# SWA's division and turning rearranged around two transposes for the last 64 keys, with narrower roots in the last norm

## The chip, the cores and the metric

The kernel runs on one core of a Trainium2 chip. The metric is the device time of one execution in microseconds. The engines are PE (TensorE, matrix products and transposes), DVE (VectorE), ACT (ScalarE), POOL (GpSimd) and SP (SyncE, which here only starts DMAs).

## The reference, cut to what matters

One step of a one-layer encoder over 1024 prompt tokens and 64 sample tokens, width 1024, in float32. The layer adds three things to the input: a mix of retention (four heads) and sliding-window attention (SWA), cross-attention to 256 memory tokens, and a SwiGLU block. A last RMS norm follows. The parts that the change touches:

```python
def swa_attend(q, k, v, bias, sinks, valid):
    s = jnp.einsum('bnqhgd,bnkhd->bnhgqk', q, k) * (SWA_HD ** -0.5) + bias
    s = jnp.where(valid, s, NEG_INF)
    m = jnp.maximum(jnp.max(s, axis=-1, keepdims=True), sink)
    e = jnp.exp(s - m)
    p = e / (jnp.sum(e, axis=-1, keepdims=True) + jnp.exp(sink - m))
    return jnp.einsum('bnhgqk,bnkhd->bnqhgd', p, v)
...
y_prompt, y_sample = rms_norm(hp, g_final), rms_norm(hs, g_final)
```

SWA has 16 query heads and 2 kv heads of 64 columns each. A chunk is 64 tokens, and its queries see 192 keys: their own chunk and the two before. Each row of exps is divided by its sum, and the weighted values follow.

## The kernel before, in words

Tokens lie along the free dimension (1088 columns), features along the 128 partitions. A product of full precision is made of three passes over high and low halves of the numbers (L156, L157, L158). The phases run one after the other: the projections and retention (to 811 us), SWA with the output projection of retention in its gaps (811 to 1007), the merge of the two branches (to 1110), cross-attention (to 1400), SwiGLU and the last norm (to 2209). A scheduler orders the instructions of each engine at build time. The code steers it with `issue_after` (this instruction stands behind that one), `in_order` (behind the last product) and, in the last norm, `queued` (DVE's instructions stand in the order of the code).

**SWA** (`swa`, L924 on). 17 chunks of 64 queries; the last is the sample's. A chunk is worked in two halves, so there are 34. The tile `t` of a half has 128 rows of queries and four blocks: two kv heads `v` by two groups of query heads `i`. From the third chunk on a block has 192 keys. A half passes through three steps.

- `scores`: products into two PSUM banks `pss` (L969). DVE adds the bias (L979, L982 in the first two chunks), takes the maximum (L984), turns it into the negative one `nm` (L985) and into the sinks' exponent `es` (L988). ACT takes four exps with their sums `den` (L990) and the sinks' (L992). DVE adds these (L993) and takes the reciprocal (L994). One POOL instruction divides all four blocks, 768 elements a partition (L996).
- `turn`: PE turns the first 128 keys of the four blocks into one bank (L1008), and ACT copies it to `pT` (L1012). PE then turns the last 64 keys in four transposes (L1018). Two of them take 64 columns, and two take 128 columns, the keys 64 to 191, to land on the upper partitions. DVE copies the result (L1020).
- `weigh`, once per chunk: four products of 512 columns (L1031), two for the first 128 keys with 128 rows by 64 columns of the array, two for the last 64 keys with 64 by 64. They add up in one bank `pout`. DVE copies it to `osb` (L1035), and SP stores that.

The order of the code is: `weigh` of the half before, `scores` of two halves ahead, `turn` of this half, and then pieces of the filler. The filler (`filler`, L1146) projects retention's output by `w_ret_out` in half pieces of 12 products. DVE multiplies a finished piece by the gate (L1187). PSUM has eight banks. The pool `pd` of the filler, which also takes the values' transposes (L946, copied by ACT at L948), has three; `pss` has two, and the two turned tiles and `pout` have one each. Weights come in by DMA as `raw` and are split into high and low by ACT (L123) and DVE (L124).

**The last norm** (`finish`, L1620). The last 16 products make the columns 0 and 1, each 272 tokens, of eight row blocks; columns 2 (544 tokens) are complete before. Per product DVE adds it to `y` (L1639), ACT squares that (L1643), and DVE gathers the squares (L1648). For the columns 2 and 0 the sums over the features come from tiny products with tokens on the partitions (`sums`, L1656), so that the roots (`steps`, L1721 to L1726) work on 5 or 3 elements a partition. PE spreads the factors over the partitions again (`spread`, L1682), and ACT copies them (L1685). For the columns 1 `wide_roots` makes the sums on all partitions at once (L1670, L1671), and the same steps work on 272 elements. Each scaling (L1689) is one DVE instruction, followed by a store from SP (L120).

## Time and profile before

| What | Value |
|---|---|
| Median of three runs | 2211.39 us (2210.66 to 2214.1) |
| The profiled execution | 2210.58 us |
| Its span | 2208.8 us |
| Mean granted clock of PE | 0.992 |
| PE busy in SWA (811 to 1007) | 186.9 of 196 us |
| DVE busy there | 143.0 us |
| POOL busy there | 53.7 us |
| PE busy from 2176 to 2208 | 16.5 of 32 us |

The profiled execution's own time is 1.8 us more than its span, the stretch from the first to the last recorded instruction. A line of the timeline has the start in us, the duration in us, the engine, the source line, the operation, the tiles written and read, the shapes and the count of the instructions drawn together. Brackets hold the idle time of the engine ahead of it and what ended that. A line of a group has the count, busy time in us and mean duration in ns.

### The profile page before, as it was taken

To read this page: it belongs to the slowest core of one execution; us is meant where nothing else is said; L and a number is where in the kernel's file an instruction comes from. 1 tells how busy PE (TensorE), PEld (TensorE's weight loads), DVE (VectorE), ACT (ScalarE), POOL (GpSimd) and SP (SyncE) were. 2 spreads that over 40 slices of the span, in tenths; PEclk is the share of its full clock that TensorE was granted. 3 is DMA by queue.
4 is the path that set the end of the run, shared out by engine and by line. 5 is a ranking of instruction groups with operands and counts; after the bars stand their busy time and mean duration, and the time that the engine had idled before them with its cause. 6 is when DMAs were issued, how large, how long until landed. Compare 5 with 4: busy or idle time off the path is not lost.

```text
span 2208.8 us, 41446 instructions
## 1 busy us (share of the span) xinstructions
PE 2155.7 (98%) x16307; PEld 2089.8 (95%) x16307; DVE 1577.8 (71%) x2654; ACT 875.8 (40%) x1894; POOL 653.2 (30%) x442
## 2 busy tenths in 40 slices
PE   8999999999999998999999999999999999999996
PEld 8999999999999996779999999999999999999996
DVE  7996958776677668775455555768777776778498
ACT  7344424344344346553133333333322222344243
POOL 1322333332343122230000000014555555544440
PEclk9999999999999999999999999999999999999998
DMA  5534253445245476327443111422333332385233
GB/s 197 167 127 137 90 149 122 131 127 156 96 153 172 165 220 213 112 64 224 124 153 107 57 49 58 144 86 90 124 133 101 104 118 95 124 297 167 91 114 110
DMA packets 181444, 290.83 MB, mean 132 GB/s; under 512 B 40290, under 2 KB 109314, under 8 KB 181250
## 3 DMA queue, kind: packets, MB, share of 16 engines
q1 hardware_dynamic: 176706, 278.74, 39.5%
q10 hardware_dynamic: 4032, 7.80, 0.9%
q8 instruction: 129, 2.11, 0.4%
q0 software_dynamic: 512, 1.64, 0.2%
q14 instruction: 65, 0.53, 0.1%
HBM read 196.95 MB, written 91.16 MB: 130 GB/s over the span
## 4 chain that ended last, share of the span: by engine, by line
PE 80%; DVE 11%; DMA 4%; ACT 2%; issue 2%; POOL 1%; SPq 0%; DVEq 0%; ACTq 0%; POOLq 0%
PE pq L215 15%; PE pq L212 15%; PE pq L213 15%; PE pd L156 8%; PE pd L158 8%; PE pd L157 8%; DVE wq L124 1%; PE pout L1031 1%; PE pss L969 1%; DMA hl<-d_op 1%; DVE T L124 1%; DVE B L124 1%; PE pp L1008 1%; DMA qs<-d_qkv 1%; DVE stage L596 1%
## 5 line engine op out<-in xcount | busy, mean ns | idle before, releaser
L124 DVE TENSOR_TENSOR wq<-raw,wq 128x512 fp32r<-128x512 f32 (+1 forms) x499 | 441.2, 888 | 137.1 <-ACT wq L123 135.5
L123 ACT CAST wq<-raw 128x512 fp32r<-128x512 f32 (+1 forms) x499 | 303.6, 614 | 586.0 <-PE pq L215 244.8
L212 PE MATMUL pq<-T,wq 128*128 128x272 f32 x1832 | 490.8, 288 | 3.6 <-ACT wq L123 2.1
L213 PE MATMUL pq<-T,wq 128*128 128x272 f32 x1832 | 491.5, 288 | 0.0
L213 PE MATMUL pq<-B,wq 128*128 128x272 f32 x1592 | 429.6, 290 | 6.7 <-DVE B L124 6.7
L212 PE MATMUL pq<-B,wq 128*128 128x272 f32 x1592 | 427.4, 289 | 1.3 <-DVE stage L596 1.1
L215 PE MATMUL pq<-T,wq 128*128 128x272 f32 x1832 | 382.0, 289 | 0.9 <-DVE wq L124 0.9
L190 POOL TENSOR_TENSOR raw<-raw 128x512 f32<-128x512 f32 (+1 forms) x59 | 90.2, 1529 | 967.1 <-DVE rs_r L301 480.4
L212 PEld LDWEIGHTS pq<-T,wq 128*128 128x128 f32 x1832 | 344.1, 188 | 5.6 <-ACT wq L123 1.9
L213 PEld LDWEIGHTS pq<-T,wq 128*128 128x128 f32 x1832 | 344.1, 188 | 0.8 <-issue 0.7
L215 PE MATMUL pq<-B,wq 128*128 128x272 f32 x1592 | 332.8, 289 | 0.0
L213 PEld LDWEIGHTS pq<-B,wq 128*128 128x128 f32 x1592 | 300.7, 189 | 9.2 <-DVE B L124 8.3
L212 PEld LDWEIGHTS pq<-B,wq 128*128 128x128 f32 x1592 | 300.5, 189 | 1.8 <-ACT wq L123 1.3
L215 PEld LDWEIGHTS pq<-T,wq 128*128 128x128 f32 x1832 | 289.6, 189 | 1.6 <-DVE wq L124 1.1
L215 PEld LDWEIGHTS pq<-B,wq 128*128 128x128 f32 x1592 | 252.8, 190 | 0.8 <-issue 0.8
L259 DVE TENSOR_TENSOR u<-pq,u 128x544 f32<-128x544 f32 x177 | 127.5, 720 | 101.3 <-PE pq L215 100.4
L193 POOL TENSOR_TENSOR raw<-raw 128x512 f32<-128x512 f32 (+1 forms) x59 | 82.8, 1403 | 110.4 <-DVE wq L124 105.3
L596 DVE TENSOR_TENSOR stage<-pq,u 128x544 f32<-128x544 f32 x112 | 80.4, 718 | 34.6 <-PE pq L215 31.2
L191 POOL TENSOR_TENSOR raw<-raw 128x512 f32<-128x512 f32 (+1 forms) x59 | 90.4, 1533 | 3.5
L996 POOL TENSOR_TENSOR t<-t,den 128x768 f32<-128x768 f32 (+2 forms) x34 | 49.9, 1468 | 127.0 <-DVE den L994 51.9
L196 POOL TENSOR_TENSOR raw<-raw 128x512 f32<-128x512 f32 (+1 forms) x59 | 82.4, 1397 | 4.4
L990 ACT ACTIVATE t<-t,nm 128x192 f32<-128x192 f32 (+2 forms) x136 | 58.9, 434 | 45.5 <-DVE nm L985 45.5
(388 smaller groups left out, 4600.4 us busy)
## 6 DMA issues: line engine op xcount, KB each, us to landing
hl<-d_op SPq DMA_DIRECT2D x85, 272.0 KB, 4.7
d_qkv<-stage SPq DMA_DIRECT2D x44, 272.0 KB, 2.2
d_op<-stage SPq DMA_DIRECT2D x44, 272.0 KB, 2.1
d_op<-ht SPq DMA_DIRECT2D x44, 272.0 KB, 3.3
raw<-w_gate SPq DMA_DIRECT2D x22, 512.0 KB, 3.5
raw<-w_up SPq DMA_DIRECT2D x22, 512.0 KB, 3.7
raw<-w_down SPq DMA_DIRECT2D x16, 512.0 KB, 4.1
d_gate<-stage ACTq DMA_DIRECT2D x28, 272.0 KB, 2.9
```

The lines of the kernel that those rows point to most:

```text
L123: self.last_cast = self.nc.scalar.copy(hi, src).ins
L124: return self.nc.vector.tensor_tensor(out=lo, in0=src, in1=hi.bitcast(F32), op=ALU.subtract).ins
L156: mm(ps, wh, xh, start=start, stop=False)
L157: mm(ps, wh, xl, start=False, stop=False)
L158: self.last_mm = mm(ps, wl, xh, start=False, stop=stop).ins
L190: tt(out=a11, in0=a11, in1=a21, op=sub)
L191: tt(out=a21, in0=a21, in1=a22, op=add)
L212: mm(ps[:, c, :HC], w[:, 0, ks], x[:, 0, cs], start=start, stop=False)
L213: mm(ps[:, c, :HC], w[:, 0, ks], x[:, 1, cs], start=False, stop=False)
L215: self.last_mm = mm(ps[:, c, :HC], w[:, 1, ks], x[:, 0, c * HC:(c + 1) * HC], start=False, stop=stop).ins
L259: add = lambda out, a, b: nc.vector.tensor_tensor(out=out, in0=a, in1=b, op=ALU.add)
L596: nc.vector.tensor_tensor(out=o, in0=ps, in1=sb, op=ALU.add)
```

## The change

**SWA.** The dense pool `pd` has two banks during SWA and three again from the merge on; `pout` has two. The division becomes three POOL instructions in a half of full width. The first takes the first 128 keys of all four blocks in place. The other two, one per kv head, take the last 64 keys and write them to a new tile `e`, in which the two kv heads lie side by side (in the second half of a chunk the other way round). Two transposes of 128 by 128 turn `e` where four turned the last 64 keys. `weigh` has four products of 256 columns for each of its two parts, and each half `h` of the columns has a bank of its own. The second part uses the four 64-by-64 quadrants of the array. In the filler, the load and the split of the third unit of `w_ret_out` stand behind the gating of the first piece.

**The last norm.** `wide_roots` goes. The sums of the columns 1 come from tiny products, and the last product's squares are added by a second product instead of a gather. The steps then work on three elements a partition, with one scaling of the columns 0 between them. The factors of the columns 0 and 1 are read where PE spread them, in PSUM. One row block of the columns 2 and three of the columns 1 get their gain from ACT and their factor from POOL (`gain`, `aside`). The last eight stores alternate between SP's and ACT's queue.

```diff
                 self.project_phase()
+                with self.plain_psum(2, side="right"):
+                    self.swa_phase()
                 with self.plain_psum(side="right"):
-                    self.mix_phase()
+                    self.merge_swa()
                     self.mem.close()
...
     @contextmanager
-    def plain_psum(self, **where):
+    def plain_psum(self, bufs=3, **where):
         with ExitStack() as ctx:
-            pd = ctx.enter_context(self.tc.tile_pool(name="pd", bufs=3, reuse_waits="tile", space=PSUM, **where))
+            pd = ctx.enter_context(self.tc.tile_pool(name="pd", bufs=bufs, reuse_waits="tile", space=PSUM, **where))
             self.dense_psum = lambda: pd.tile([P, 512], F32, tag="d", name="pd")
...
 
-    def mix_phase(self):
+    def swa_phase(self):
         with ExitStack() as ctx:
...
             self.swa(ctx, fill())
-        self.merge_swa()
 
...
                 nc.vector.reciprocal(den, den)
-                p = lambda x: x.rearrange("p v i n -> p (v i) n")
-                nc.gpsimd.tensor_tensor(out=p(t)[:, :, :nk], in0=p(t)[:, :, :nk], op=ALU.mult,
-                                        in1=den.rearrange("p v i -> p (v i)").unsqueeze(2).broadcast_to([P, 4, nk]))
-                live[c, hf] = t
+                p, n, e = t.rearrange("p v i n -> p (v i) n")[:, :, :min(nk, P)], min(nk, P), None
+                nc.gpsimd.tensor_tensor(out=p, in0=p, op=ALU.mult,
+                                        in1=den.rearrange("p v i -> p (v i)").unsqueeze(2).broadcast_to([P, 4, n]))
+                if nk == NKEY:
+                    e = sw.tile([P, 2, 2, 64], F32, tag="e", bufs=4, name="e")
+                    for v in range(2):
+                        nc.gpsimd.tensor_tensor(out=e[:, :, v ^ hf, :], in0=t[:, v, :, P:], op=ALU.mult,
+                                                in1=den[:, v, :].unsqueeze(2).broadcast_to([P, 2, 64]))
+                live[c, hf] = t, e
 
...
                     live[c] = [values(ks + k0) for k0 in ((0, 64, P) if nk == NKEY else (0,))]
-                t, vt = live.pop((c, hf)), live[c]
+                (t, e), vt = live.pop((c, hf)), live[c]
                 n = min(P, nk)
...
                 nc.scalar.copy(pT[:, :, hf * 256:(hf + 1) * 256], pp[:n, :].rearrange("p (v i) -> p v i", v=2))
-                parts = [[(vt[0][:n], pT[:, v, :]) for v in range(2)]]
+                cs = [slice(h * 256, (h + 1) * 256) for h in range(2)]
+                parts = [[(h, v, vt[0][:n], pT[:, v, cs[h]]) for h in range(2) for v in range(2)]]
                 if nk == NKEY:
                     pp = pw.tile([P, 512], F32, tag="pt1", name="pp")
-                    for v, i in reversed(units):
-                        k0, n = (64, P) if v else (P, 64)
-                        self.last_mm = nc.tensor.transpose(pp[:n, i * P:(i + 1) * P], t[:, v, i, k0:k0 + n], self.ident).ins
+                    for i in range(2):
+                        x = e[:, i].rearrange("p r k -> p (r k)")
+                        self.last_mm = nc.tensor.transpose(pp[:, i * P:(i + 1) * P], x, self.ident).ins
                     pT = live[c, "T"][1]
                     nc.vector.tensor_copy(pT[:, hf * 256:(hf + 1) * 256], pp[:, :256])
-                    parts.append([(vt[2 - v][rows[v]], pT[rows[v]]) for v in range(2)])
+                    parts.append([(h, r ^ h, vt[2 - r][rows[r]], pT[rows[r], cs[h]]) for h in range(2) for r in (h, 1 - h)])
                 live[c, "parts"] = parts
...
                 parts = live.pop((c, "parts"))
-                po = pw.tile([P, 512], F32, tag="out", name="pout")
+                po = pw.tile([P, 2, 512], F32, tag="out", name="pout")
                 for j, part in enumerate(parts):
-                    for v, (val, pT) in enumerate(part):
-                        self.last_mm = mm(po[rows[v], :], val[:, rows[v]], pT, start=j == 0, stop=j == len(parts) - 1).ins
+                    for h, v, val, pT in part:
+                        self.last_mm = mm(po[rows[v], h, :256], val[:, rows[v]], pT, start=j == 0, stop=j == len(parts) - 1).ins
                 if c % 2 == 0:
...
                 osb = outs["osb"]
-                nc.vector.tensor_copy(osb[:, :, c % 2, :], po.rearrange("p (m q) -> p m q", q=64))
+                nc.vector.tensor_copy(osb[:, :, c % 2, :].rearrange("p (h m) q -> p h m q", h=2),
+                                      po[:, :, :256].rearrange("p h (m q) -> p h m q", q=64))
                 if c % 2 == 1 or c == 16:
...
                 if m not in units:
-                    units[m] = self.unit(io["w_ret_out"][m], KT)
+                    if m == 2:
+                        with tc.issue_after(first):
+                            units[m] = self.unit(io["w_ret_out"][m], KT)
+                    else:
+                        units[m] = self.unit(io["w_ret_out"][m], KT)
                 u, g = units[m], ld()
...
                         yield
-                nc.vector.tensor_tensor(out=g[:, :n], in0=ps, in1=g[:, :n], op=ALU.mult)
+                ins = nc.vector.tensor_tensor(out=g[:, :n], in0=ps, in1=g[:, :n], op=ALU.mult).ins
+                if step == 2:
+                    first = ins
                 self.store(self.d_mix[m, :, c0:c0 + n], g[:, :n])
...
 
-        def sums(c):
+        def sums(c, *more):
 
...
             ps = bank()[:, :2 * len(spans)].rearrange("p (t two) -> p t two", two=2)
+            parts = [self.rstd[:, cols[c]], *more]
             for i, (a, w) in enumerate(spans):
-                a += cols[c].start
-                self.last_mm = nc.tensor.matmul(ps[:, i, :], self.rstd[:, a:a + w], self.ones[:, :2], start=True, stop=True).ins
+                for j, x in enumerate(parts):
+                    self.last_mm = nc.tensor.matmul(ps[:, i, :], x[:, a:a + w], self.ones[:, :2], start=j == 0,
+                                                    stop=j == len(parts) - 1).ins
             r = self.np.tile([P, 5], F32, tag="rf", bufs=2, name="rs_f")[:, :len(spans)]
...
 
-        def roots(c):
+        def roots(c, between=None):
             r, spans, ps = factors[c]
...
             t = self.np.tile([P, 5], F32, tag="tf", bufs=2, name="rf_t")[:, :len(spans)]
-            self.steps(r, v, t, ps)
-
-        def wide_roots(c, m):
+            self.steps(r, v, t, ps, between)
 
-            ps = bank()[:, :HC]
-            mm = nc.tensor.matmul
-            mm(ps, self.ones, self.rstd[:, cols[c]], start=True, stop=False)
-            self.last_mm = mm(ps, self.ones, squares[c, m], start=False, stop=True).ins
-            v, t = (self.hl.tile([P, HALF], F32, tag="hl", name="wide")[:, :HC] for _ in range(2))
-            self.steps(self.rstd[:, cols[c]], v, t, ps)
-
-        def spread(c):
+        def spread(c, copied=True):
             r, spans, _ = factors[c]
...
                 c0 = cols[c].start
-                nc.scalar.copy(self.rstd[:, c0 + a0:c0 + a1], pb[:, :a1 - a0])
+                if copied:
+                    nc.scalar.copy(self.rstd[:, c0 + a0:c0 + a1], pb[:, :a1 - a0])
+            return pb
+
+        def scale(c, k, by=None, queue=nc.sync):
+            o = y[k][:, cols[c]]
+            by = self.rstd[:, cols[c]] if by is None else by
+            self.queued(lambda: stt(o, o, self.gains[:, 3, k:k + 1], by, ALU.mult, ALU.mult))
+            queue.dma_start(self.io["o_y"][k, :, cols[c]], o)
 
-        def scale(c, k):
+        def gain(c, k):
             o = y[k][:, cols[c]]
-            self.queued(lambda: stt(o, o, self.gains[:, 3, k:k + 1], self.rstd[:, cols[c]], ALU.mult, ALU.mult))
-            self.store(self.io["o_y"][k, :, cols[c]], o)
+            nc.scalar.mul(o, o, self.gains[:, 3, k:k + 1])
+
+        def aside(c, k, queue=nc.sync):
+            o = y[k][:, cols[c]]
+            nc.gpsimd.tensor_tensor(out=o, in0=o, in1=self.rstd[:, cols[c]], op=ALU.mult)
+            queue.dma_start(self.io["o_y"][k, :, cols[c]], o)
 
...
             if j == KT + 6:
-                self.in_order(lambda: spread(0))
-            if j >= KT:
-                scale(2, j - KT)
-        for k in range(3):
-            scale(0, k)
-        self.in_order(lambda: wide_roots(1, rest[-1][0]))
+                pb0 = self.in_order(lambda: spread(0, False))[:, :HC]
+            if c and m < KT - 1:
+                scale(2, m)
+            if c and KT - 5 < m < KT - 1:
+                gain(1, rest[m][0])
+            if j == 2 * KT - 2:
+                gain(2, KT - 1)
+                aside(2, KT - 1)
+        m = rest[-1][0]
+        spare = [rest[i][0] for i in range(KT - 4, KT - 1)]
+        scale(0, 0, pb0)
+        scale(0, 1, pb0)
+        self.in_order(lambda: sums(1, squares[1, m]))
+        roots(1, lambda: scale(0, 2, pb0))
         for k in range(3, KT):
-            scale(0, k)
-        for k in range(KT):
-            scale(1, k)
+            scale(0, k, pb0)
+        pb = self.in_order(lambda: spread(1))[:, :HC]
+        queues = [nc.sync, nc.scalar]
+        rows = [k for k in range(KT) if k not in spare]
+        for i, k in zip((2, 4, 7), spare):
+            rows.insert(i, k)
+        for i, k in enumerate(rows):
+            if k in spare:
+                aside(1, k, queues[i % 2])
+            else:
+                scale(1, k, pb, queues[i % 2])
 
-    def steps(self, out, v, t, ps):
+    def steps(self, out, v, t, ps, between=None):
         nc = self.nc
...
         nc.scalar.activation(out, v, AF.Sqrt)
+        if between is not None:
+            between()
         q(lambda: nc.vector.reciprocal(out, out))
```

In the built order of the instructions, POOL has three instructions per half of full width instead of one, PE two transposes instead of four and eight products per `weigh` instead of four. L1187 of the first piece stands ahead of the two splits of the third unit on DVE, and the transposes of the last values (L946) stand behind the last `turn`. In the merge, the first products that read the seventh operand stand six products earlier on PE. DVE's order within a chunk is as it was.

## The prediction

> **What bounds the kernel now.** The page comes first, for the bound of the whole.
>
> ```profile
> span 2208.8 us, 41446 instructions
> ## 1 busy us (share of the span) xinstructions
> PE 2155.7 (98%) x16307; PEld 2089.8 (95%) x16307; DVE 1577.8 (71%) x2654; ACT 875.8 (40%) x1894; POOL 653.2 (30%) x442
> ```
>
> PE is busy for 98% of the span. A change pays only if it takes PE time away, or time in which PE has nothing to do. Two stages matter, so the busy times by stretch come next: the steady part of the sliding-window attention (SWA), and the tail behind the last product.
>
> ```profile
> 880.00:1000.00 120.00, 120.00 (x788) 90.67 (x787) 86.48 (x194) 65.92 (x253) 34.83 (x23) 1.00 0.30 92
> 2193.00:2208.00 15.00, 1.18 (x4) 0.68 (x4) 11.32 (x24) 0.86 (x2) 0.00 (x0) 0.59 0.54 186
> ```
>
> The columns are the stretch, its length, then PE, PEld, DVE, ACT and POOL busy, the granted clock and the DMA share. From 880 to 1000 PE never stops, while DVE works 86.5 of 120 us and POOL 34.8. From 2193 on PE does 1.18 us in 15 and DVE sets the time. The copy of the weighted values, once per chunk, gives the period of the loop:
>
> ```profile
> L1035 DVE COPY osb<-pout x12: 680/692/693, 881.5 to 993.7; 128x512 f32<-128x512 f32 x12
> ```
>
> Twelve copies, 112.2 us from first to last: 10.2 us per chunk of two halves, bound by PE.
>
> **SWA, what PE saves.** The timeline of PE at one turn:
>
> ```profile
> 908.90 2.09 PE L1031 MATMUL pout<-pT,swin 128*64 128x512 f32 x8
> 910.92 0.92 PE L969 MATMUL pss<-swin,swin 64*128 64x192 f32 x8
> 911.77 0.33 PE L946 MATMUL pd<-ident,swin 128*128 128x128 f32 x1
> 911.94 0.60 PE L1008 MATMUL pp<-ident,t 128*128 128x128 f32 x4
> 912.37 0.60 PE L1018 MATMUL pp<-ident,t 128*128 128x128 f32 x4
> 912.73 0.42 PE L156 MATMUL pd<-ret,wq 128*128 128x384 f32 x1
> ```
>
> Four transposes of L1008 take 0.43 us from start to start (911.94 to 912.37), so one is 0.11, and two fewer in L1018 save 0.22 per half, 0.44 per chunk. The weighing takes 2.02 us (908.90 to 910.92) in two parts of 1.01, each two tiles side by side. The second part becomes four products of 256 columns on the four 64x64 quadrants. If they run two by two, they cost what they cost now, or up to 0.2 more if each start costs as between these rows; if all four run at once the part falls by 0.43. PE alone would so allow 10.2 − 0.44 = 9.76 us per chunk, or 9.33.
>
> At this place a rule of the Trainium skill speaks against the sum (TensorEngine Tiling (Array Packing), Restrictions and Gotchas): different row tiles may not use one PSUM bank at the same time. The two tiles of the second part before are of different row halves, write one bank, and yet took 1.01 us for two passes of 512 columns each, as the first part did; the trace doesn't show the rule for different partitions of a bank. After, each half of the columns has a bank of its own. By the rule the second part would run two by two; without it, all four.
>
> **SWA, what the loop allows.** The last-64-key transposes now wait for the third of three POOL operations. Prices of the division:
>
> ```profile
> L996 POOL TENSOR_TENSOR t<-t,den 128x768 f32<-128x768 f32 x30 | 45.6, 1521 | 106.8 <-DVE den L994 34.3 <-DVE nm L985 30.1 <-PE pss L969 17.9
> L996 POOL TENSOR_TENSOR t<-t,den 128x512 f32<-128x512 f32 x2 | 2.4, 1192 | 15.0 <-DVE den L994 15.0
> L996 POOL TENSOR_TENSOR t<-t,den 128x256 f32<-128x256 f32 x2 | 1.9, 947 | 5.2 <-DVE den L994 2.7 <-DVE es L988 2.6
> ```
>
> 256 elements cost 0.95, 512 cost 1.19, 768 cost 1.47 undisturbed: about 1.08 ns an element on 0.64 us. An operation of 128 elements isn't in the trace; between nothing less than the 0.64 and the 0.95 of 256, I take 0.77, on the line. The three are then 1.19 + 2 × 0.77 = 2.73 us, with gaps some 2.84, against 1.47: 1.4 later than now.
>
> ```profile
> 904.84 0.45 ACT L990 ACTIVATE t<-t,nm 128x192 f32<-128x192 f32 x1 [1.37 <-DVE nm L985]
> ...
> 908.44 1.73 POOL L996 TENSOR_TENSOR t<-t,den 128x768 f32<-128x768 f32 x1 [4.54 <-DVE den L994]
> ...
> 908.76 1.43 DVE L985 SCALAR_TENSOR_TENSOR nm<-nm,minus 128x4 f32<-128x4 f32 x1
> ...
> 914.99 0.46 ACT L990 ACTIVATE t<-t,nm 128x192 f32<-128x192 f32 x1 [1.77 <-DVE nm L985]
> ```
>
> The loop of one half: exps (904.84) to the division (908.44) are 3.60; the three operations 2.84; then the second transposes, the copy L1020, and behind it on DVE L984, L985 and the exps of the half two later, 2.62 us (912.37 to 914.99). Sum 9.06 us, below the 9.76 of PE, without one thing: L985, with two inputs in SBUF, took 1.43 us instead of about 0.16 (914.73, in the rows after these, started 0.26 ahead of its exps) and ended at 910.19, just when POOL did (908.44 + 1.73 = 910.17). So a DVE operation of two SBUF inputs waits for a POOL operation that is running. Does it wait for all three? Here is a waiting one with a second POOL operation queued:
>
> ```profile
> 325.25 1.30 POOL L191 TENSOR_TENSOR raw<-raw 128x512 f32<-128x512 f32 x1
> ...
> 325.86 1.24 DVE L124 TENSOR_TENSOR wq<-raw,wq 128x512 fp32r<-128x512 f32 x1 [0.58 <-ACT wq L123]
> ...
> 326.51 1.81 POOL L602 TENSOR_TENSOR stage<-stage,rstd 128x544 f32<-128x544 f32 x1
> ```
>
> L191 ends at 326.55, L124 at 327.10 and L602 at 328.32: DVE got in between, and POOL waited. So L985 waits at most for the one that runs, 0 to 1.19; with hits in about a third of the chunks' time I add 0.4: loop 9.5, still below 9.76. The Trainium skill says the same of the lock (SBUF — State Buffer, Who interferes with whom): it is held for one instruction, and the other blocks. I take PE as the bound with a small part of the quadrants' overlap: 0.5 us per chunk (between −0.2 and 0.87), **12 chunks, −6.0**. The first chunks are bound by other things and get nothing.
>
> **SWA, the edges.** At halves 4 and 33 nothing lies between the division and the turn:
>
> ```profile
> 848.63 1.47 POOL L996 TENSOR_TENSOR t<-t,den 128x768 f32<-128x768 f32 x1 [4.11 <-DVE den L994]
> ...
> 850.15 0.66 PE L1008 MATMUL pp<-ident,t 128*128 128x128 f32 x4
> ...
> 995.48 1.47 POOL L996 TENSOR_TENSOR t<-t,den 128x768 f32<-128x768 f32 x1 [2.65 <-DVE den L994]
> ...
> 997.00 0.66 PE L1008 MATMUL pp<-ident,t 128*128 128x128 f32 x4
> ```
>
> The second transposes come 0.43 behind L1008, at 850.59 and 997.44; after, they could start at 848.63 + 2.84 + 0.05 = 851.52 and 998.37. **+0.9 each, +1.9.** Behind them in PE's queue stands the filler, which waits with them.
>
> The dense pool has two tiles instead of three, so a piece waits for the copy of the piece before the last. Once per some pieces that is late:
>
> ```profile
> 914.89 0.34 PE L156 MATMUL pd<-ret,wq 128*128 128x384 f32 x1
> ...
> 915.09 0.56 DVE L1187 TENSOR_TENSOR swin<-pd,swin 128x384 f32<-128x384 f32 x1
> ```
>
> This piece starts 0.8 before the other has been read (915.65). Four tiles of 38 are late in this way, by 0.3 to 0.8: **+1.5** (0.5 to 3).
>
> At the start PE stands 4.0 us, because DVE's queue waits for weights:
>
> ```profile
> PE pss L969 <- DVE t L982: 4.0, 1, 4.0
> ```
> ```profile
> 829.71 1.14 ACT L123 CAST wq<-raw 128x512 fp32r<-128x512 f32 x2 [7.25 <-DMA raw<-w_ret_out]
> ...
> 831.57 0.55 DVE L1187 TENSOR_TENSOR swin<-pd,swin 128x384 f32<-128x384 f32 x1
> ```
>
> L1187 of the first piece moves ahead of the splits that wait for that cast, so L982 behind it comes 0.55 earlier: **−0.5**. The casts on ACT stay where they are, so the wait itself remains.
>
> In the merge the scheduler puts the products with the seventh SWA operand 6 matmuls earlier. Its cast comes just in time now:
>
> ```profile
> 1027.58 1.86 ACT L123 CAST swa<-ld 128x320 fp32r<-128x320 f32 x4 [2.41 <-DMA ld<-d_swa]
> ...
> 1028.92 0.69 PE L156 MATMUL pd<-swa,wq 128*128 128x384 f32 x3
> ```
>
> Six matmuls are 1.0 us at 0.17 each: **+0.8** (0 to 1.5). SWA in sum: −6.0 + 1.9 + 1.5 − 0.5 + 0.8 = **−2.3**.
>
> **The finish.** Narrow factors as the trace shows them for columns 0, then the wide ones and the scales:
>
> ```profile
> 2185.33 0.73 PE L1656 MATMUL pq<-ones,rstd 128*128 128x2 f32 x6
> ...
> 2186.71 0.16 DVE L1721 TENSOR_SCALAR rf_v<-pq 128x3 f32<-128x3 f32 x1
> ...
> 2187.75 0.16 DVE L1726 SCALAR_TENSOR_TENSOR rs_f<-rf_t,rs_f 128x3 f32<-128x3 f32 x1
> ```
> ```profile
> 2193.55 0.73 PE L1670 MATMUL pq<-rstd,ones 128*128 128x272 f32 x2 [2.18 <-DVE rstd L1648]
> ...
> 2195.34 0.44 DVE L1721 TENSOR_SCALAR wide<-pq 128x272 f32<-128x272 f32 x1
> ...
> 2199.12 0.44 DVE L1726 SCALAR_TENSOR_TENSOR rstd<-wide,rstd 128x272 f32<-128x272 f32 x1
> 2199.48 2.15 DVE L1689 SCALAR_TENSOR_TENSOR y<-y,gains,rstd 128x272 f32<-128x272 f32 x5
> ...
> 2202.88 3.38 SPq L120 DMA_DIRECT2D o_y<-y  x7
> ```
>
> Before: sums from 2193.55, roots 2195.34 to 2199.56, then 13 scales at 0.41 (five in 2.15 less the last's overlap), the last store issued by 2206, the end 2.9 later. After: the sums start by 2193.8 (POOL's `aside` of (2,7) holds one L1648 by the lock, 0.3 to 0.5), twelve tiny products cost 2 × 0.73, so the roots start at 2195.4; the narrow steps take 1.2 (2186.71 to 2187.91), with one scale between them 1.7 to 1.9: 2197.3. The spread is 3 tiny products and the wait, 0.9: 2198.2. Beside it DVE does the other five scales of columns 0, 2197.3 to 2199.35. Left are five scales with the factor in PSUM, 2.1 us, to 2201.5; three rows go to POOL at some 0.93 each (272 elements on the line above) from 2198.8, when ACT's copy is there, to 2201.7. Two queues issue the stores, 0.48 each (3.38 for 7), so the last goes at 2201.8 and the end comes 2.9 later at 2204.7 instead of 2208.8: **−4.1** (−2.5 to −5.0). That a DVE scale with its factor in PSUM costs no more than one in SBUF isn't shown; L1639, which reads PSUM, takes the same 0.44 for 272 elements. The lower end is for POOL being held by DVE.
>
> **Sum.** −2.3 − 4.1 = −6.4 on the profiled execution's 2210.6 gives 2204.2. That execution lay 0.8 below the median of 2211.4, so **2205**.
>
> **Rivals.** (a) All four quadrants run at once and the second transposes are never late: 0.87 per chunk, −10.4 for SWA's loop; with the rest unchanged −10.8, 2200.6, and 2196 if the first chunks gain too. For it: two column tiles and two row tiles each do run side by side in the rows above. Against it: the loop of 9.5 would then be longer than PE's 9.33. (b) The new weighing costs its starts (0.2 per chunk) or the loop eats the saving, and the two-buffer and merge terms are at their upper ends: −3 + 1.9 + 3 − 0.5 + 1.5 − 4.1 = about −1, and with a finish of −2.5 about 0: 2208 to 2212. In this case the change does what it says, and the saved transposes don't arrive on the path. (c) Slower: the lock. If L985 waits for all of the POOL operations behind each other, not for one, each loop gets 1.27 more, and L993, of two SBUF inputs too, 0.77: 9.06 + 2.04 = 11.1, which is 0.9 above today's 10.2. Then the loop's term is +10.8 instead of −6.0: 2222. It decides from a loop of 10.6 on (12 × 0.4 = 4.8, which with +3.7 of edges and −4.1 of the finish is 4.4). Against it stand the rows at 325 us.
>
> **Chances.** Forecast (2201.5 to 2207) 0.52, (a) 0.20, (b) 0.17, (c) 0.11. The range 2197 to 2213 leaves out (c) and the far end of (a). A measurement of this kernel can tell about 0.2%, 4.4 us, from no change: faster means below 2207.0, slower above 2215.8. Faster holds (a) and nearly all of the forecast, 0.68; same 0.21; slower 0.11.
>
> **What the profile after would show.** The two L1018 transposes at 0.11 each and a period of L1035 near 9.7; L985 at 0.16 or up to 1.2, never 2; the sum of the three divisions near 2.8; no PE wait on POOL's `e` but at two halves; PE's waits for L1187 or L948 summing to about 1.5; the second part of the weighing at 1.0 (two by two) or 0.55 (four). In the finish, the narrow L1721 near 2195.4, the last DVE scale near 2201.5, the end 4 us earlier. The forecast falls if PE waits for POOL or L1020 in every chunk, or if the tail's last store goes out later than 2203.

## The result, and the profile after

The changed kernel takes 2199.95 us (median of four runs, 2197.7 to 2201.3) against 2212.1 us for the kernel before, whose four runs lie between 2210.66 and 2214.1. The ratio is 0.9937, with a 95% interval of 0.9925 to 0.9949. The forecast was 2205, with a range of 2197 to 2213; the time lies in the range and 5 us below the forecast, at what rival (a) gave, 2200.6.

The page of the changed kernel, in the same lines as before:

```profile
span 2198.7 us, 41701 instructions
## 1 busy us (share of the span) xinstructions
PE 2151.3 (98%) x16389; PEld 2096.3 (95%) x16389; DVE 1566.3 (71%) x2650; ACT 877.2 (40%) x1898; POOL 658.1 (30%) x506
```

The span is 10.1 us shorter, and PE is as full as it was. The busy times of the steady part of SWA, in the columns of the prediction, and the copy that counts its chunks:

```profile
880.00:1000.00 120.00, 120.00 (x894) 98.77 (x893) 83.61 (x199) 67.28 (x250) 42.30 (x69) 1.00 0.34 102
```
```profile
L1042 DVE COPY osb<-pout x12: 683/692/692, 879.0 to 982.4; 128x512 f32<-128x512 f32 x12
```

PE still never stops. POOL works 42.3 instead of 34.8 us. Twelve copies now lie 103.4 us from first to last instead of 112.2, so a chunk takes 9.4 instead of 10.2 us.

One turn on PE, with the columns start, duration, engine, line, tiles, shapes and count:

```profile
895.37 1.68 PE L1038 MATMUL pout<-pT,swin 128*64 128x256 f32 x16
896.98 0.92 PE L970 MATMUL pss<-swin,swin 64*128 64x192 f32 x8
897.83 0.33 PE L947 MATMUL pd<-ident,swin 128*128 128x128 f32 x1
898.00 0.60 PE L1014 MATMUL pp<-ident,t 128*128 128x128 f32 x4
898.43 0.38 PE L1025 MATMUL pp<-ident,e 128*128 128x128 f32 x2
898.57 0.40 PE L156 MATMUL pd<-ret,wq 128*128 128x320 f32 x1
```

From start to start, the weighing takes 1.61 us (895.37 to 896.98) instead of 2.02, although it has twice the instructions. The transposes of the last 64 keys take 0.14 us (898.43 to 898.57) instead of 0.36 (912.37 to 912.73).

What the three divisions cost:

```profile
L997 POOL TENSOR_TENSOR t<-t,den 128x512 f32<-128x512 f32 x32 | 35.2, 1100 | 97.4 <-DVE nm L986 26.4 <-DVE den L995 19.8 <-DVE es L989 18.2
L1002 POOL TENSOR_TENSOR e<-t,den 128x128 f32<-128x128 f32 x60 | 24.9, 432 | 0.0
```
```profile
L1002 POOL TENSOR_TENSOR e<-t,den x60: 389/397/920, 849.4 to 984.7; 128x128 f32<-128x128 f32 x60
```

An operation of 128 elements takes 0.40 us (median) and not 0.77, and the first one 1.04 undisturbed and not 1.19. All three are 1.8 us. But the same instruction of 512 elements in chunk 1, which has no `e`, takes 1.19 and 1.21 us here too:

```profile
840.93 1.21 POOL L997 TENSOR_TENSOR t<-t,den 128x512 f32<-128x512 f32 x1 [2.45 <-DVE den L995]
```

PE's waits from the start of SWA to the merge:

```profile
PE pss L970 <- DVE t L983: 3.7, 2, 2.2
PE pd L156 <- ACT swa L123: 1.2, 1, 1.2
PE pp L1014 <- POOL t L997: 0.8, 1, 0.8
PE pout L1038 <- ACT pT L1018: 0.6, 1, 0.6
PE pp L1025 <- POOL e L1002: 0.3, 1, 0.3
```

The stand of 2.2 us is that of the scores of half 3 (halves are counted from 0; the expectations call them the third scores). The second transposes wait for `e` once, for 0.3 us. No wait for a bank of the dense pool is in the list. The merge waits 1.2 us for a cast of its operand, which it did not do before.

**Where the time went.** The stretches below are cut at the first score product, the first product of each output projection, the first and last Strassen product of SwiGLU (L212 to L215), and the last product of the kernel. In the middle columns each kernel is given by its one profiled execution, in us; PE's period is the distance of the scores of half 10 and half 32, divided by eleven chunks.

| Kernel | start of SWA | SWA | w_swa_out | to SwiGLU | SwiGLU | tail | PE's period | ratio to before, 95% |
|---|---|---|---|---|---|---|---|---|
| before | 811.5 | 208.5 | 94.9 | 358.9 | 694.0 | 17.7 | 10.36 | |
| changed | 813.2 | 193.8 | 97.3 | 360.0 | 697.1 | 14.1 | 9.56 | 0.9925 to 0.9949 |
| swa_only | 811.3 | 193.0 | 98.6 | 358.9 | 695.1 | 17.7 | 9.55 | 0.9920 to 0.9950 |
| finish_only | 814.5 | 207.7 | 95.5 | 358.9 | 695.4 | 14.0 | 10.36 | 0.9981 to 1.0008 |
| two_quadrants | 814.0 | 200.7 | 95.7 | 360.0 | 697.2 | 14.2 | 9.92 | 0.9937 to 0.9966 |
| four_turns | 818.4 | 202.1 | 96.6 | 358.9 | 698.3 | 15.1 | 9.95 | 0.9960 to 0.9982 |
| late_one | 816.9 | 196.5 | 95.7 | 358.9 | 695.2 | 14.7 | 9.67 | 0.9924 to 0.9955 |
| late_two | 811.6 | 210.7 | 96.3 | 359.0 | 694.9 | 14.2 | 10.17 | 0.9988 to 1.0005 |
| one_bank_three | 810.9 | 198.4 | 95.9 | 358.8 | 695.9 | 14.6 | 9.92 | 0.9926 to 0.9953 |
| hold_four | 811.2 | 195.5 | 97.1 | 358.9 | 697.1 | 15.8 | 9.04 | 0.9928 to 0.9954 |
| no_order | 812.3 | 198.8 | 95.7 | 358.8 | 696.1 | 14.1 | 9.56 | 0.9923 to 0.9964 |
| warm | 816.9 | 193.9 | 95.6 | 358.8 | 695.2 | 14.1 | 9.56 | 0.9919 to 0.9957 |
| dve_scales | 810.0 | 194.0 | 97.4 | 360.1 | 694.4 | 14.2 | 9.56 | 0.9901 to 0.9938 |
| dve_again | 815.9 | 194.2 | 95.3 | 358.7 | 694.5 | 15.5 | 9.56 | 0.9907 to 0.9945 |

Between before and changed, SWA gives 14.7 us and the tail 3.6. The phases ahead of SWA take 1.8 back, the first projection of the merge 2.4, the stretch behind it 1.1 and SwiGLU 3.1. The code ahead of SWA and in SwiGLU is the same in all fourteen kernels, and their times there spread over 810 to 818 and 694 to 698. Of the merge's 2.4, 1.2 are the wait, and the rest is a slower spacing of the products, which comes and goes in kernels of the same code (last section). So a time of one kernel can be off by several us for a reason that has nothing to do with the change, and the stretches tell more than the medians. By their times, only `finish_only`, `four_turns` and `late_two` can be told from the changed kernel; the intervals of the others overlap with its own. `one_bank_three`, whose SWA is 4.6 us longer in the trace, has a ratio of 0.9939 against 0.9937. What is said below of these variants rests on one trace each. The period of PE is the sharpest: 9.55 to 9.56 in six kernels that share this SWA loop, 10.36 in both that have the old one.

### The profile page after: what moved, and what is told of

Read it like the earlier page. It is cut to its first block, busy times and chain, and to the rows that moved or that the text cites. A ratio compares the mean times of both kernels' runs of the same rounds, so it can differ in the third digit from the quotient of the medians.

```text
span 2198.7 us, 41701 instructions
## 1 busy us (share of the span) xinstructions
PE 2151.3 (98%) x16389; PEld 2096.3 (95%) x16389; DVE 1566.3 (71%) x2650; ACT 877.2 (40%) x1898; POOL 658.1 (30%) x506
## 4 chain that ended last, share of the span: by engine, by line
PE 77%; DVE 11%; DMA 5%; issue 3%; ACT 3%; POOL 1%; SPq 0%; POOLq 0%; DVEq 0%; ACTq 0%
PE pq L215 15%; PE pq L213 15%; PE pq L212 15%; PE pd L156 7%; PE pd L158 7%; PE pd L157 7%; DVE wq L124 2%; DMA hl<-d_op 1%; PE pout L1038 1%; DVE T L124 1%; DVE B L124 1%; PE pss L970 1%; DMA raw<-w_k 1%; PE pp L1014 1%; DMA qs<-d_qkv 1%
## 5 line engine op out<-in xcount | busy, mean ns | idle before, releaser
L212 PE MATMUL pq<-T,wq 128*128 128x272 f32 x1832 | 491.7, 288 | 4.5 <-ACT wq L123 3.1
L212 PE MATMUL pq<-B,wq 128*128 128x272 f32 x1592 | 427.6, 289 | 2.3 <-DVE stage L598 2.0
L215 PE MATMUL pq<-T,wq 128*128 128x272 f32 x1832 | 382.9, 289 | 0.0
L190 POOL TENSOR_TENSOR raw<-raw 128x512 f32<-128x512 f32 (+1 forms) x59 | 79.0, 1339 | 968.7 <-DVE rs_r L301 482.9
L212 PEld LDWEIGHTS pq<-T,wq 128*128 128x128 f32 x1832 | 344.9, 188 | 6.5 <-ACT wq L123 2.9
L215 PE MATMUL pq<-B,wq 128*128 128x272 f32 x1592 | 333.4, 290 | 0.0
L213 PEld LDWEIGHTS pq<-B,wq 128*128 128x128 f32 x1592 | 300.9, 189 | 10.6 <-DVE B L124 9.7
L212 PEld LDWEIGHTS pq<-B,wq 128*128 128x128 f32 x1592 | 300.4, 189 | 3.2 <-ACT wq L123 2.7
L215 PEld LDWEIGHTS pq<-T,wq 128*128 128x128 f32 x1832 | 290.5, 190 | 0.5 <-issue 0.3
L215 PEld LDWEIGHTS pq<-B,wq 128*128 128x128 f32 x1592 | 253.4, 190 | 0.8 <-issue 0.8
L193 POOL TENSOR_TENSOR raw<-raw 128x512 f32<-128x512 f32 (+1 forms) x59 | 83.5, 1415 | 125.7 <-DVE wq L124 120.6
L191 POOL TENSOR_TENSOR raw<-raw 128x512 f32<-128x512 f32 (+1 forms) x59 | 90.8, 1539 | 3.5
L196 POOL TENSOR_TENSOR raw<-raw 128x512 f32<-128x512 f32 (+1 forms) x59 | 83.0, 1406 | 4.4
L1486 POOL TENSOR_TENSOR stage<-stage,rstd_f 128x544 f32<-128x544 f32 x40 | 63.9, 1607 | 39.1 <-ACT stage L1485 39.1
L156 PE MATMUL pd<-xc,wq 128*128 128x256 f32 (+1 forms) x256 | 74.5, 291 | 0.0
```

The costliest lines, as they stand in the source:

```text
L156: mm(ps, wh, xh, start=start, stop=False)
L191: tt(out=a21, in0=a21, in1=a22, op=add)
L193: tt(out=a11, in0=a22, in1=a11, op=sub)
L196: tt(out=a12, in0=a12, in1=a11, op=sub)
L212: mm(ps[:, c, :HC], w[:, 0, ks], x[:, 0, cs], start=start, stop=False)
L213: mm(ps[:, c, :HC], w[:, 0, ks], x[:, 1, cs], start=False, stop=False)
```

## The experiments

The theory after the result: PE bounds SWA before and after, and each chunk loses the 0.44 us of four transposes and the 0.41 us of four quadrants working at once. The rivals: a good part of the gain comes from the last norm, or the loop of exps, division and turn sets the period.

**One part of the change alone.** `swa_only` has the new SWA and the old `finish`; `finish_only` has the old SWA and the new `finish`.

> The SWA part of the change alone, with the last norm of before. Theory (SWA is bound by PE, and each chunk loses the 0.44 us of four transposes and the 0.41 us of the quadrants): between the first scores and the first product of the merge the profiled SWA is 14.7 us shorter than before, of which the merge gives 2.4 back by a wait and a slower spacing of its products; the time is 8 to 11 us below before, and the period of the copy of the weighted values is 9.4 us. The rival (a good part of the gain stands in the last norm, 7 us or more): only 4 to 6 us below before.

> The last norm of the change alone, with the SWA of before. Theory: the stretch from the last product to the end shrinks by 3.6 us, 2207 to 2209 us in all, and SWA stands as before. The rival: the tail gains nothing by itself but through what lies ahead of it, and the time is within 1 us of before.

Measured: 2200.38 us (ratio 0.9935) with SWA alone, a tail as before, 17.7 us, and SWA at 193.0. With the last norm alone 2212.7 us against 2214.31 for before in the same runs (ratio 0.9994), a tail of 14.0 and SWA at 207.7. SWA gives nearly all of the measured gain. The 3.6 us of the tail stand clearly in the trace of `finish_only`, but 0.16% lies inside the interval of its ratio, so the time can't show them. The merge's loss was larger in `swa_only` than expected:

```profile
1005.00:1011.60 6.60, 6.60 (x40) 6.60 (x39) 3.65 (x8) 2.65 (x6) 0.00 (x0) 1.00 0.82 247
1011.60:1014.10 2.50, 0.42 (x4) 0.10 (x2) 0.52 (x2) 1.03 (x3) 0.00 (x0) 0.98 0.99 365
1014.10:1017.60 3.50, 3.50 (x11) 3.50 (x12) 2.46 (x6) 1.56 (x4) 0.00 (x0) 0.52 0.89 279
1017.60:1040.00 22.40, 22.40 (x139) 22.40 (x138) 13.41 (x25) 5.97 (x11) 0.00 (x0) 1.00 0.60 184
```

The columns are those of the stretches in the prediction; the last three are the granted clock, the DMA share and GB/s. PE stands 2.1 us for its operand while the DMA engines are 99% busy, and then runs eleven products in 3.5 us at a granted clock of 0.52: in this run the wait costs its length once and about 1.5 us more behind it (ten distances of 0.32 instead of 0.17). `hold_four` below shows a wait of the same length without that.

**The quadrants.** `two_quadrants` keeps the kv heads in place in both halves, so that the second part of the weighing uses the same two quadrants for both halves of the columns:

```diff
-                        nc.gpsimd.tensor_tensor(out=e[:, :, v ^ hf, :], in0=t[:, v, :, P:], op=ALU.mult,
+                        nc.gpsimd.tensor_tensor(out=e[:, :, v, :], in0=t[:, v, :, P:], op=ALU.mult,
...
-                    parts.append([(h, r ^ h, vt[2 - r][rows[r]], pT[rows[r], cs[h]]) for h in range(2) for r in (h, 1 - h)])
+                    parts.append([(h, r, vt[2 - r][rows[r]], pT[rows[r], cs[h]]) for h in range(2) for r in range(2)])
```

> As the changed kernel, but the kv heads keep their place in e in both halves, so that the second part of the weighing uses two of the 64 by 64 quadrants for both halves of the columns. Theory (four quadrants at once are worth 0.41 us a chunk): the weighing takes 2.0 instead of 1.6 us, the period 9.75 instead of 9.34, 15 chunks, 6 us slower than the changed kernel. The rival (loop of exps, division and turn is the bound, the weighing hides): no slower than the changed kernel by more than 1.5 us.

The weighing and what follows it on PE in this kernel:

```profile
889.33 2.10 PE L1038 MATMUL pout<-pT,swin 128*64 128x256 f32 x16
891.35 0.92 PE L970 MATMUL pss<-swin,swin 64*128 64x192 f32 x8
```

The same sixteen instructions of the same shapes take 2.02 us here and 1.61 in the changed kernel. The only difference is which quadrants the second part uses. PE's period grows by 0.37 us, SWA by 6.9. Of these, 1.6 stand at the scores of half 3, up to which both kernels run the same code; the other 5.3 fit 15 chunks at 0.37. So the four quadrants do work at once when each half of the columns has its own bank. Doubling the number of instructions costs nothing: eight of 512 columns took 2.02 us too.

**The transposes.** `four_turns` issues the two new transposes twice:

```diff
-                    for i in range(2):
-                        x = e[:, i].rearrange("p r k -> p (r k)")
-                        self.last_mm = nc.tensor.transpose(pp[:, i * P:(i + 1) * P], x, self.ident).ins
+                    for j in range(4):
+                        x = e[:, j % 2].rearrange("p r k -> p (r k)")
+                        self.last_mm = nc.tensor.transpose(pp[:, j * P:(j + 1) * P], x, self.ident).ins
```

> As the changed kernel, but the two transposes of the last 64 keys are issued twice, so that PE has four again. Theory (PE is the bound): 0.22 us a half for 30 halves, 6.5 us slower than the changed kernel. The rival (the loop is the bound): within 1.5 us of the changed kernel.

PE's period is 9.95, 0.39 more, and SWA is 8.3 us longer. Half by half the scores fall back by 0.21 to 0.22 us through the steady part, the price of two transposes. The 1.8 us beyond the theory stand at halves 9 and 10, where other waits fell differently. The rival, a bound by the loop, is out in both runs.

**The loop's reserve.** `late_one` adds one POOL operation of 430 elements to a division, `late_two` two of 600, which read `t` and write a tile that nobody reads:

```diff
                 if nk == NKEY:
+                    x = sw.tile([P, 430], F32, tag="late", bufs=1, name="late")
+                    nc.gpsimd.tensor_tensor(out=x, in0=t.rearrange("p v i n -> p (v i n)")[:, :430], op=ALU.mult,
+                                            in1=den[:, 0, :1].broadcast_to([P, 430]))
                     e = sw.tile([P, 2, 2, 64], F32, tag="e", bufs=4, name="e")
```

> As the changed kernel, with one POOL operation of 430 elements more between the division of the first 128 keys and that of the last 64 (it reads t and writes a tile that nobody reads). It brings the three divisions, measured at 1.04 + 2 x 0.39, to the 2.7 us that the prediction had priced. Theory (PE is the bound and has about 1.2 us to spare in the loop): the period of the copy of the weighted values stays at 9.4 us, and the waits of the second transposes for e stay at the first and the last halves; within 3 us of the changed kernel. The rival (the loop decides, by late transposes or by VectorE's small operations behind POOL): a period of 9.8 us or more, 6 us slower.

> As the changed kernel, with two POOL operations of 600 elements more at that place, about 2.4 us: 4.2 us of division in all. Theory (a loop of exps to division 2.5 to 3.6, division, and turn to exps 2.6): 9.3 to 10.4 us, so the loop takes over in part, the period is 9.6 to 10.4, and PE waits for e in most chunks; 4 to 15 us slower than the changed kernel. The rival (PE stays the bound whatever POOL takes): a period of 9.4 us and waits at the edges only.

The scheduler did not keep that place. In `late_one` the added operation runs behind the two that write `e`, and in `late_two` mostly:

```profile
893.98 1.04 POOL L997 TENSOR_TENSOR t<-t,den 128x512 f32<-128x512 f32 x1 [0.67 <-DVE den L995]
894.98 0.76 POOL L1005 TENSOR_TENSOR e<-t,den 128x128 f32<-128x128 f32 x2
895.69 0.90 POOL L1001 TENSOR_TENSOR late<-t,den 128x430 f32<-128x430 f32 x1
```

So these runs do not test a late `e` by itself. They test a POOL that is busy for 2.7 or 4.2 us per half, with all that stands behind it. At 2.7 us PE's period rises by 0.11 to 9.67, but all of it, 1.2 us, falls on two halves (22 and 23) of the eleven chunks, and the other halves lose nothing; SWA is 2.7 us longer. At 4.2 us the period is 10.17. PE waits for POOL twelve times, six of them for `e`, which was expected in most chunks:

```profile
PE pp L1020 <- POOL t L997: 4.2, 6, 1.2
PE pss L970 <- DVE t L983: 4.0, 2, 2.5
PE pp L1031 <- POOL e L1008: 2.9, 6, 1.1
PE pss L970 <- DVE t L980: 2.9, 2, 1.9
```

The small operation on `nm` shows how VectorE is held, in the changed kernel, `late_one` and `late_two` in turn (minimum, median and maximum in ns):

```profile
L986 DVE SCALAR_TENSOR_TENSOR nm<-nm,minus x21: 161/163/166, 882.4 to 976.5; 128x4 f32<-128x4 f32 x21
```
```profile
L986 DVE SCALAR_TENSOR_TENSOR nm<-nm,minus x21: 161/165/715, 881.5 to 976.4; 128x4 f32<-128x4 f32 x21
```
```profile
L986 DVE SCALAR_TENSOR_TENSOR nm<-nm,minus x20: 148/320/997, 882.1 to 978.7; 128x4 f32<-128x4 f32 x20
```

In the changed kernel it never waits; in the other two it waits up to 0.55 and 0.83 us, less than one POOL operation lasts (0.90 and 1.19). Of VectorE's other two small operations with two inputs in SBUF, from 882 to 976 us, `den` (L994) never waits in the changed kernel and `es` (L989) once, for 0.89 us; in `late_two` they wait up to 0.91 and 0.95. The theory holds in kind: with the POOL time that the prediction had priced, the loop delays PE in one place, and with 2.4 us more than in the changed kernel it delays it in many.

These runs also show what an operation on POOL costs in the steady part, here in `late_two`:

```profile
891.88 1.07 POOL L997 TENSOR_TENSOR t<-t,den 128x512 f32<-128x512 f32 x1 [2.43 <-DVE nm L986]
...
903.85 1.18 POOL L1001 TENSOR_TENSOR late<-t,den 128x600 f32<-128x600 f32 x1
904.99 1.03 POOL L997 TENSOR_TENSOR t<-t,den 128x512 f32<-128x512 f32 x1
```

The operation of 512 elements takes 1.07 us behind 2.43 us of idle time and 1.03 directly behind another, so its place in a row is worth next to nothing. The medians of 0.40 (128), 0.90 (430), 1.04 (512) and 1.18 (600), and the 1.47 of before (768, undisturbed and alone), lie on one line: 0.18 us and 1.67 ns an element. The operations of the first two chunks lie above it: 256 elements took 0.95 there instead of 0.61, and 512 took 1.19 instead of 1.04. Why is open.

**The two dense buffers.** `one_bank_three` weighs with two quadrants as two products of 512 columns into one bank, and gives the bank that comes free to the dense pool, which has three tiles again:

```diff
-                with self.plain_psum(2, side="right"):
+                with self.plain_psum(3, side="right"):
...
-                po = pw.tile([P, 2, 512], F32, tag="out", name="pout")
+                po = pw.tile([P, 512], F32, tag="out", name="pout")
```

> As the kernel with two quadrants, but its second part is two products of 512 columns into one bank, and the bank that comes free goes to the dense pool, which has three again. Theory (two dense buffers cost 0.5 to 3 us, as predicted): SWA's stretch, from the first scores to the first product of the merge, is 199 us against 200.7 of the kernel with two quadrants. The rival (two buffers cost nothing that shows): 200.2 to 201.2.

SWA's stretch is 198.4 against 200.7 of `two_quadrants`, 2.3 us less, as the theory had it; but the pair does not show that the buffers are the reason. The period is 9.92 in both, so two buffers cost nothing in the loop. The whole difference stands in the first eight halves, most of it at the scores of half 3, where the weights' DMA sets the time. These come 19.1 us behind the first scores in `one_bank_three` and 21.8 in `two_quadrants`. But the ten kernels that have two buffers and the new order, and the same code up to there, spread from 19.5 to 21.8, and `two_quadrants` is the latest of them. So most of the 2.3 can be scatter.

**The order of the third unit.** `no_order` takes the `issue_after` of the filler away:

```diff
-                    if m == 2:
-                        with tc.issue_after(first):
-                            units[m] = self.unit(io["w_ret_out"][m], KT)
-                    else:
-                        units[m] = self.unit(io["w_ret_out"][m], KT)
+                    units[m] = self.unit(io["w_ret_out"][m], KT)
```

> As the changed kernel, but the third unit of w_ret_out is loaded and split without standing behind the gating of the first piece, as before. Theory (that order shortens the stand of PE at the third scores from 4.0 to 2.2 us): the wait of the scores for L982's counterpart is 1.6 us longer, and SWA's stretch 195.4 instead of 193.8. The rival (the wait is for the weights' DMA, which comes when it comes): SWA's stretch within 0.7 us of the changed kernel.

SWA is 198.8 us, 5.0 longer, three times what the theory gave, and the wait is another. The scores of half 3 come 25.0 us behind the first, 3.2 later than in the latest of the ten kernels with the order, so this is more than their scatter:

```profile
PE pd L156 <- DVE swin L1195: 5.5, 1, 5.5
PE pss L970 <- DVE t L983: 1.5, 1, 1.5
```

With two dense tiles the next piece can't start until DVE has gated the first, and that gating (L1195 here) stands on DVE's queue behind splits that wait for the weights. With three tiles, as before, PE came as far as the scores and stood there 4.0 us. So the order and the two buffers belong together: the order is what makes two buffers cheap at the start.

**More filler behind the loop.** `hold_four` moves four half pieces of the filler behind the last weighing, to cover the merge's loads:

```diff
-                count, steps, done = 48 - 10, 2 * 17, 0
+                count, steps, done = 48 - 14, 2 * 17, 0
...
-                yield [pieces] * 8
+                yield [pieces] * 12
```

> As the changed kernel, but four half pieces of the filler more stand behind the last weighing (12 instead of 8), so that four fewer stand in the chunks. Theory (SWA now ends before the loads of its own result for the merge have come): the wait of the merge's products for the cast of swa, 1.2 us, goes, the merge's first products take 95 us instead of 97, SWA's stretch stays at 194; 2 to 4 us faster in these stages. The rival (the chunks with less filler are bound by the loop, or the loads start later too): SWA's stretch grows by as much, and nothing is won.

The theory fell. SWA grew by 1.7 us, and the merge waited longer:

```profile
PE pd L156 <- ACT swa L123: 2.1, 1, 2.1
```

The loads did start earlier (984.2 against 992.9), but three casts of the second group of columns came only at 1013.8, behind the last store of the filler, so the merge's wait was 2.1 us instead of 1.2. Which buffer held them was not tried. This wait is as long as that of `swa_only`, but behind it PE runs twenty products in 3.5 us at a granted clock of 1.00:

```profile
1014.30:1017.80 3.50, 3.47 (x20) 3.47 (x21) 2.75 (x6) 1.11 (x3) 0.00 (x0) 1.00 0.53 164
```

The run shows one thing more: with less filler PE's period is 9.04 us, so the loop of exps, division and turn takes at most 9.04.

**The tail.** `warm` adds products that nobody reads, five of 272 columns ahead of the last sums and two ahead of the last spread. `dve_scales` gives all eight scalings of the columns 1 to VectorE (`spare = []`, and no `gain` for them).

> As the changed kernel, with seven products of 272 columns that nobody reads, five ahead of the tiny sums of the columns 1 and two ahead of their spread, so that PE isn't idle there. Theory (PE's clock falls in the idle time behind the last product, and the six products of the spread, 1.65 us instead of 0.83, pay for it): the spread takes 0.8 to 1.0 us, and the tail, from the last product to the end, 13.3 us instead of 14.1; by the time itself not to be told from the changed kernel. The rival (the spread is slow for another reason): 1.6 us and a tail of 14.1.

> As the changed kernel, but VectorE scales all eight row blocks of the columns 1, none goes by ACT and POOL. Theory (the narrow roots are the larger part of the 3.6 us of the new last norm, and the three blocks on POOL hide 1.2 us of scales): a tail of 15.0 to 15.5 us against 14.1 of the changed kernel and 17.7 of before. The rival (POOL's blocks and the two queues make the gain): 16.5 us or more. A third (POOL's three blocks end as late as VectorE's eight would): 14.1.

The tail of the changed kernel first, on PE, DVE and POOL:

```profile
2190.09 1.65 PE L1689 MATMUL pq<-ident,rs_f 128*128 128x128 f32 x6 [1.33 <-DVE rs_f L1763]
```
```profile
2188.80 0.16 DVE L1756 TENSOR_SCALAR rf_v<-pq 128x3 f32<-128x3 f32 x1 [0.78 <-PE pq L1671]
...
2189.95 2.12 DVE L1699 SCALAR_TENSOR_TENSOR y<-y,gains,pq 128x272 f32<-128x272 f32 x5
2192.20 0.50 DVE L1699 SCALAR_TENSOR_TENSOR rstd_f<-rstd_f,gains,pq 128x272 f32<-128x272 f32 x1
2192.61 1.72 DVE L1699 SCALAR_TENSOR_TENSOR y<-y,gains,pq 128x272 f32<-128x272 f32 x4
```
```profile
2192.24 2.19 POOL L1708 TENSOR_TENSOR y<-y,rstd 128x272 f32<-128x272 f32 x3 [15.85 <-ACT rstd L1693]
```

The spread in `warm`:

```profile
2189.09 0.93 PE L1699 MATMUL pq<-ident,rs_f 128*128 128x128 f32 x6 [0.30 <-DVE rs_f L1773]
```

The added products do what they should: the granted clock stays at 1.00 where it was 0.50, and the spread takes 0.93 us instead of 1.65. But the tail stays at 14.12 us. In `dve_scales` VectorE works until 2189.97, 11.0 us behind its last product, and in the changed kernel until 2194.33, 9.7 behind; yet both tails are 14.1 to 14.2 us, the third outcome of those expected. What does bound it, the DMA view of the changed kernel from 2191 to 2196 shows, in 40 slices of 0.125 us (9 is 90% or more busy):

```profile
DMA  0049988998799659957994599999999999999999
```

From 2193.9 on the engines are full, at some 360 GB/s. Before the change the last stores went out from one queue, one each 0.49 us, at 270 to 300 GB/s. In the changed kernel the last eight stores of 136 KB are issued by 2195.2, 10.6 us behind the last product; in `warm` by 10.3 and in `dve_scales` by 11.3, and all three kernels end within 0.05 us of each other. The stores leave as fast as DMA takes them, and a store that is issued earlier only waits longer. So neither the help of POOL and ACT nor the clock of the spread shows a gain here; each stands on one trace. What is left of the new last norm, the narrow steps, the factors read from PSUM and the second queue, brought the stores forward; these were not taken apart.

**A faster variant?** The time of `dve_scales`, 2196.5 us, was the lowest of all, so it was run once more.

> The kernel with all eight scalings of the columns 1 on VectorE once more, with more rounds. Its first time, 2196.5 us, lay 3.5 us below the changed kernel's, but its tail was the same 14.16 us, and the difference stood in the phases ahead of SWA (3.3 us) and in SwiGLU (2.8 us), whose code is the same. Theory (scatter of those phases): about 2200 us and a ratio near 0.994, a tail of 14.1 to 14.2. The rival (a real gain): at most 2197.5 us and a ratio of 0.992 again, with SwiGLU near 694 us.

2197.98 us, with a ratio of 0.9926 (0.9907 to 0.9945), between the two outcomes. The tail was 15.5 us this time, though VectorE's last scale again ended 11.0 us behind the last product, so the 1.3 us more stand in the stores; over the twelve kernels with the new last norm the tail lies between 14.0 and 15.8. SwiGLU took 694.5 us again, while the other kernels with the new last norm have 694.9 to 698.3, and the kernel before 694.0. The intervals overlap with the changed kernel's, so it stays open whether this variant gains some 2 us in SwiGLU, where its code is the same, or whether that is scatter. No kernel of the study is clearly faster than the changed one.

## Why the prediction was right, and where it was off

- **The bound.** PE bounds SWA before and after, as forecast; the period fell by what PE saved.
- **Transposes, 0.44 us per chunk.** This was right: the scores fall back by 0.22 us per half in `four_turns`, and the transposes take 0.14 instead of 0.36 us per turn.
- **The quadrants, −0.43 or nothing.** The step took "a small part of the quadrants' overlap". They overlap in full: the weighing takes 1.61 instead of 2.02 us. The Trainium skill (TensorEngine Tiling (Array Packing), Restrictions and Gotchas) says that different row tiles may not use one PSUM bank at the same time. As it stands this does not agree with the runs: two row tiles that wrote different partitions of one bank ran side by side before and in `two_quadrants` (2.02 us for the weighing), and in the changed kernel two such pairs, each in its own bank, ran at once (1.61). Row tiles in the same partitions of a bank, and four quadrants in one bank, were not tried.
- **Three divisions, 2.73 us.** This is the step that failed. It put 128 elements on the line through 256, 512 and 768, at 0.77 us; the trace has 0.40, half of it. The 256 and the 512 came from the first two chunks alone, where an operation takes longer than later (1.19 us for 512 and not 1.04), so the line was too flat and its base of 0.64 too high; in the steady part it is 0.18 us and 1.67 ns an element. That a short operation is cheap because it follows another is not the reason, as the rows of `late_two` show. The three divisions are 1.8 us, 0.35 more than the one before and not 1.3. So the loop that was put at 9.5 us is at most 9.04 (`hold_four`), and the reason for staying at −0.5 per chunk, against the −0.87 of rival (a), was not there. Even a loop of 9.5 would have left 0.7 of today's 10.2, so the 0.5 was cautious beyond the prediction's own sum. `late_one`, whose POOL is busy for the 2.7 us of the forecast, loses 0.11 per chunk on average, and that in one place; but its added operation does not delay `e`.
- **The lock.** VectorE waits for the running POOL operation and not for the row of them: the longest wait of its small operations was 0.95 us, in `late_two`, where a row takes 4.2. Of the 0.4 us per chunk nothing was paid by `nm` in the changed kernel; `es` waited once. Rival (c) did not happen. In `late_two`, with 4.2 us of POOL per half, the ratio to before is 0.9988 to 1.0005, no slower than before.
- **Halves 4 and 33, +1.9.** PE waits 0.3 us for `e` at half 4 and not at all at half 33; the same price was at fault.
- **Two buffers, +1.5 over four tiles.** Nothing of it shows in the loop: from 840 us on PE never waits for a dense bank in the changed kernel. At the start no more shows than the scatter of kernels with the same code there. The term is not borne out.
- **Start, −0.5.** The stand at the scores of half 3 fell from 4.0 to 2.2 us, but this is not all due to the change: it was 3.0 us in `finish_only`, which has the old SWA, and 3.1 in `two_quadrants`, which has the new order. Once there are two buffers the order is worth 3 to 5 us (`no_order`).
- **Merge, +0.8.** The wait came where forecast, with 1.2 us; in kernels with the same SWA it was between nothing (`dve_again`) and 2.1 (`swa_only`), and 0.4 in `finish_only`. What follows it was not foreseen: products at half clock, or a slower spacing.
- **Finish, −4.1.** The tail fell by 3.6 us. The roots began at 2188.80, 4.2 us behind the last product as before (2195.34 − 2191.08 = 4.3), so the gain lies behind them. The step "the last goes at 2201.8 and the end comes 2.9 later" failed: the end is 3.6 us behind the last issue, because the DMA engines are full and not the queues. The three rows on POOL took 0.73 us each where the same line of prices had given 0.93.

The loop gave 0.80 us per chunk where 0.5 was forecast, and it did so in some 15 chunks and not 12: about 12 us instead of 6, which is more than the 5 us by which the median lies below the forecast; the halves 4 and 33 and the start were better too, and the merge and the phases whose code is the same took a part back. Rival (a), at 0.20, is what happened. That the median lies only 5 us below the forecast is in part luck: SWA gained 14.7 us in the trace, and 6.0 of the gains went in the phases ahead of SWA, behind the merge's first projection and in SwiGLU, where the code is the same.

## What to carry to other kernels

When an engine is full and its neighbours have room, ask first what a change takes from that engine; then measure how far the loop of the others lies below it, for instance by moving work out of the loop, before a forecast is held back for its sake. Price a short operation by a line through operations of the steady part, and see first whether those of the first passes lie on it. And cut a run into stretches: in kernels with the same code, PE's period agrees here to 0.01 us and SWA to 1.2, where the phases ahead of SWA spread over 8. Compare the scatter of a stretch over such kernels with a difference before it is given a cause.

## What the runs showed of the hardware that was not expected

- In the steady part of SWA a POOL operation took 0.18 us and 1.67 ns for each element of a partition (128 to 768 elements), alone or directly behind another; 256 elements in the first chunk took 0.95 us, more than the 0.76 of two operations of 128 later.
- Sixteen matrix instructions of 256 columns took 1.61 or 2.02 us by the quadrants that they used, all else equal.
- Behind a stand of 2.1 us PE ran eleven products in 3.5 us at a granted clock of 0.52 (`swa_only`); behind another of 2.1 us (`hold_four`) and one of 1.15 (the changed kernel) it ran twenty at 1.00. So the length of the stand alone does not decide it. In the changed kernel another thing began there: the products of 384 columns followed each other at 176.7 ns instead of 173.3 to the end of the merge's projections. The rows of one stretch in before and in the changed kernel, minimum, median and maximum in ns:

```profile
L158 PE MATMUL pd<-swa,wq x9: 309/334/337, 1055.5 to 1059.6; 128*128 128x384 f32 x8, 128*128 128x320 f32 x1
```
```profile
L158 PE MATMUL pd<-swa,wq x9: 308/338/341, 1056.2 to 1060.4; 128*128 128x384 f32 x8, 128*128 128x320 f32 x1
```

  It is 2%, 1.1 to 1.3 us for each of the two projections, at a granted clock of 1.00. `dve_scales` had it to the end too. The kernel before had the same slow spacing in its first two pieces and lost it in the third; five others had it for one to four pieces, and six not at all. Why it comes and goes is open.
- The changed kernel's last stores, from two queues, are bound by DMA at some 360 GB/s, whoever computes what they carry.
